# Counted V chunks of a mixture layer: all in rounded halves, twenty-two closing rows, first row reads one by one

## The chip, the cores and the metric

The program runs on one core of a Trainium2 chip. What is measured is the device time of one execution in microseconds (us); the time of a kernel is the median of several runs. The engines are TensorE (PE, with its weight loads as PEld), VectorE (DVE), ScalarE (ACT), GpSimd (POOL) and SyncE (SP, which here only issues transfers). The core has 16 DMA engines.

## The reference

One encoder layer on 256 tokens of width 2048 and one final norm. The change touches only the last sublayer and the end of the program: PEER, a mixture of 16,384 single-neuron experts. Eight product-key heads choose 16 experts each per token; an expert is a row u of one table and a row v of another:

```python
def block(args):
    xb, eb, gb = args
    u = u_tab[eb]
    act = jax.nn.gelu(jnp.einsum('td,tkd->tk', xb, u).astype(jnp.float32))
    return jnp.einsum('tk,tkd->td', (gb * act).astype(xb.dtype), v_tab[eb])
...
h = h + peer_ffn(rms_norm(h, ffn_norm_g), peer_w_q, peer_sub_keys, peer_u, peer_v)
...
return rms_norm(h, final_norm_g)
```

So a token's result is the sum over its 128 experts of gate x gelu(u . x) x v, added to h, and then normed.

## The kernel before

The retention and recurrent groups, the cross-attention and the routing fill the first half of the program. The expert layer is done in two ways at once. **Dense:** some experts are computed for all 256 tokens on TensorE, with gates that are zero where a token did not choose them: 40 rows of 128 experts fixed by number (U and V, in NCH = 5 chunks of 8 columns of 128 experts) and 32 columns of 128 that the kernel counts as the most chosen (the *counted* columns, NDY = 4 chunks, numbers 5 to 8; their rows are fetched from the tables by index, through `dyn`). **By row:** what is left of a token's choice, 38 rows for each of the two token halves (BASE = 38, tt = 0 and 1), is gathered by index: one transfer of 128 x 2048 f32 (1 MB) brings one row for each of 128 tokens. VectorE takes the dot products with u (`dot`, line 1508) and later accumulates coefficient x v into the output `hh` (`axpy`, line 1516). Choices that overflow the 38 are packed into two spill rows.

**The dense part** is one list of steps that `run` works through: U steps for all chunks, then V chunks in the order ORDER = (0, 1, 2, 3, 5, 6, 7, 8, 4). The last of them, chunk 4, is done by `v_final`. A V step normally works in rounded halves: ScalarE casts 1024 columns of the weight row to a reduced f32 form (`hi`, line 1422), VectorE forms the rest (`lo`, line 1442), and TensorE does three products, activations-hi x hi, activations-lo x hi and activations-hi x lo (`r_mms`, lines 1243, 1244 and 1246, for a counted chunk). The activations are split in the same way ahead of the chunk (`prep_steps`: `rounded` on ScalarE, line 1360, `left` on VectorE, line 1364, two of each per chunk). Chunks named in PLAIN skip all of that: `p_mms` (line 1252) multiplies the f32 activations with the f32 row as it came. There are four buffers `hi` and three `lo`. `given(n)` hands the activation buffer of a chunk that is through to the readers of counted rows (`rows_v`) or to the gathers (`ring`).

**The row work** runs beside the steps: after each step `wv.pump(rate)` adds a credit, and the generator `chosen` spends 2.2 of it per row. The rate is RP = 2.0 for a plain step and RR = 1.3 for a rounded step of a counted chunk. Of the 76 accumulations the last END, all of tt = 1, are set aside as *closing* rows: `ending` gives them out in `v_final`, whose loop of 12 tiles takes 18, between TensorE's products of chunk 4. The sums of TensorE's accumulators into `hh` are line 1694 (`added`, three quarters of the width) and line 1728 (the last quarter, once per token half, after TensorE's last product of that half); then the norm: squares on ScalarE (line 1670), a product with the gain on GpSimd (1719) and VectorE (1731), a reduction and a reciprocal root (1732, 217 to 224), a scaling (1740 on VectorE, 1736 on ScalarE) and the output's transfers.

**First reads.** While the last U columns of the early chunks run (line 164), VectorE finishes the choice of columns and rows (`compact`). When the second token half has been looked up, `first_reads` (line 1040) puts five transfers of 1 MB in a row on GpSimd's queue: the first normed rows `hn` into h[0], the first three counted U rows (two `row` tiles and h[1]), and the second normed rows into `held_in[8]`, which is `kept[3]`. Three gathers for the row work (`ahead`) were issued just before. The copies of one column ahead of each read (line 1044) tie the read to VectorE's order. After that come the products that pack the spill rows (`off`, line 1081; `spill`, line 1110, twice), and `rest()`, a branch on the chip for tokens that overflow further.

All engines work their instructions off in a fixed order, which the scheduler sets from the order in which the code was written and its own costs, except in stretches under `manual_schedule` (the steps, and the closing loop).

## Time and profile before

| | |
|---|---|
| median of 3 runs | 1923.39 us (1921.18 to 1926.32) |
| the profiled execution | 1924.19 us, span 1922.4 us, mean granted clock 0.990 |
| TensorE / VectorE / ScalarE / GpSimd busy | 97% / 80% / 45% / 29% of the span |
| first reads on GpSimd's queue | 1165.7 to 1179.5 us from the span's start |
| chunk 5 (plain), TensorE | 1665.4 to 1720.4 us |
| chunk 4 with the closing rows | from 1850.97 us |
| TensorE's last product ends | about 1912.8 us |

Times in the prediction's rows are microseconds from the span's start. A timeline row gives start, length, engine, line, instruction, output<-inputs, shape, count, and in brackets how long the engine had been idle before it and what released it. A row of a group gives busy us and mean ns of one, then the idle time before them. Line numbers are those of before unless "after" is said; from line 1040 on, after's numbers are two higher through most of the code (lines 1042 to 1110 differ by up to three).

### The profile page before, as it was taken

The page shows a single profiled execution, that of the slowest core. Times are in us where ns is not written, and L with a number is a line of the kernel's source. Part 1 is how long each engine was busy: PE and PEld are TensorE (multiplying, and loading weights), DVE is VectorE, ACT ScalarE, POOL GpSimd, SP SyncE. Part 2 cuts the span into 40 slices and gives each one's busy share as a digit, 9 for nine tenths or more (in the row PEclk, how much of TensorE's full clock was granted, in tenths as well). Part 3 has the DMA queues.
Part 4 walks back from the last instruction along what each step waited for, and adds up shares of the span by engine and source line. Part 5 has one row for each costly group of instructions (what it writes and reads, how often), then busy time and mean ns, then how long its engine had stood idle before and what let it go on. Part 6 is the DMA issues. An engine that isn't in the chain of part 4 may idle for free.

```text
span 1922.4 us, 28682 instructions
## 1 busy us (share of the span) xinstructions
PE 1871.8 (97%) x10698; PEld 1590.8 (83%) x10698; DVE 1529.1 (80%) x2336; ACT 871.9 (45%) x1340; POOL 550.7 (29%) x372
## 2 busy tenths in 40 slices
PE   9999999999999999999999998899999999899997
PEld 8888888888888988889999998888988787558863
DVE  6877979754556655799998887799999998689976
ACT  6567444544455555555347761333333433214411
POOL 0200010000000000000004641455553777388852
PEclk9999999999999999999999998999999999999999
DMA  8775665466665446855567999799898999899993
GB/s 286 287 214 170 214 212 168 155 184 192 194 180 165 149 154 187 294 166 175 200 220 175 189 245 314 269 372 387 305 408 319 353 393 412 327 367 398 420 411 134
DMA packets 202815, 498.03 MB, mean 259 GB/s; under 512 B 107040, under 2 KB 112800, under 8 KB 174624
## 3 DMA queue, kind: packets, MB, share of 16 engines
q1 hardware_dynamic: 163552, 261.57, 43.8%
q0 software_dynamic: 36384, 225.61, 29.8%
q10 hardware_dynamic: 2736, 8.99, 1.3%
q8 instruction: 84, 1.38, 0.3%
q14 instruction: 59, 0.48, 0.1%
HBM read 505.34 MB, written 21.04 MB: 274 GB/s over the span
## 4 chain that ended last, share of the span: by engine, by line
PE 68%; DMA 14%; DVE 9%; issue 5%; POOL 2%; ACT 1%; SPq 0%; POOLq 0%; DVEq 0%; ACTq 0%
PE wb L153 9%; PE xc L206 7%; PE xc L207 7%; PE xc L209 7%; PE wb L155 5%; PE U L164 5%; DMA gs<-in_Us_dram,idx 4%; PE acc L1252 3%; PE acc L1688 3%; PE G L1180 3%; DVE lo L144 3%; DMA kept<-in_V_dram 3%; DMA h<-in_Us_dram,dyn 2%; PE acc L1243 2%; PE acc L1244 2%
## 5 line engine op out<-in xcount | busy, mean ns | idle before, releaser
L144 DVE TENSOR_TENSOR lo<-raw,hi 128x1024 fp32r<-128x1024 f32 x364 | 443.8, 1221 | 213.1 <-PE xc L209 120.7
L143 ACT CAST hi<-raw 128x1024 fp32r<-128x1024 f32 x364 | 381.8, 1052 | 372.5 <-PE xc L207 170.9
L164 PE MATMUL U<-xn,hi 128*128 128x256 f32 x1280 | 176.4, 290 | 7.7 <-ACT hi L143 7.7
L164 PEld LDWEIGHTS U<-xn,hi 128*128 128x128 f32 x1280 | 164.4, 197 | 8.6 <-ACT hi L143 8.6
L804 POOL DMA_DIRECT2D hn<-h x2 | 1.1, 561 | 508.6 <-DVE h L802 508.6
L153 PE MATMUL U<-xn,hi 128*128 128x512 f32 x512 | 139.1, 404 | 0.2 <-DVE foldu L1285 0.2
L1422 ACT CAST hi<-kept 128x1024 fp32r<-128x1024 f32 x58 | 60.5, 1053 | 137.1 <-DMA at<-in_Vs_dram,idx 45.9
L153 PE MATMUL wb<-hT,hi 128*128 128x512 f32 x448 | 116.9, 396 | 0.5 <-ACT hi L143 0.5
L1167 POOL TENSOR_TENSOR kept<-kept 128x512 f32<-128x512 bf16 x64 | 73.9, 1155 | 108.4 <-DVE kept L1166 107.9
L153 PEld LDWEIGHTS U<-xn,hi 128*128 128x128 f32 x512 | 92.0, 190 | 15.7 <-DVE foldu L1285 0.5
L1508 DVE SCALAR_TENSOR_TENSOR junk<-gs,h 128x2048 bf16<-128x2048 f32 x43 | 98.2, 2283 | 6.4 <-DMA gs<-in_Us_dram,idx 6.2
L164 PE MATMUL U<-xn,lo 128*128 128x256 f32 x640 | 92.2, 287 | 4.9 <-DVE lo L144 4.7
L153 PEld LDWEIGHTS wb<-hT,hi 128*128 128x128 f32 x448 | 80.6, 189 | 14.7 <-ACT hi L143 0.7
L153 PE MATMUL wb<-xT,hi 128*128 128x512 f32 x352 | 89.2, 394 | 0.2 <-ACT hi L143 0.2
L164 PEld LDWEIGHTS U<-xn,lo 128*128 128x128 f32 x640 | 82.8, 193 | 7.7 <-DVE lo L144 7.3
L1439 DVE TENSOR_TENSOR lo<-uT,hi 128x512 fp32r<-128x512 f32 x128 | 81.9, 682 | 8.1 <-ACT hi L1420 7.2
L1501 POOL DMA_INDIRECT gs<-in_Us_dram,idx x51 | 60.0, 1177 | 79.1 <-DVE junk L1508 71.8
L1166 DVE TENSOR_TENSOR kept<-kept,kept 128x512 bf16<-128x512 bf16 x128 | 75.3, 636 | 7.5 <-PE cnt L1183 6.7
L1230 PE MATMUL acc<-hi,xe 128*128 128x512 f32 x192 | 77.7, 405 | 3.2 <-ACT hi L1422 3.1
L1516 DVE SCALAR_TENSOR_TENSOR hh<-gs,coef,hh 128x2048 f32<-128x2048 f32 x30 | 70.5, 2350 | 8.3 <-DMA gs<-in_Vs_dram,idx 8.1
L1442 DVE TENSOR_TENSOR lo<-kept,hi 128x1024 fp32r<-128x1024 f32 x58 | 69.6, 1221 | 9.3 <-ACT hi L1422 6.2
L1231 PE MATMUL acc<-hi,xe 128*128 128x512 f32 x192 | 77.0, 401 | 0.0
(532 smaller groups left out, 4603.9 us busy)
## 6 DMA issues: line engine op xcount, KB each, us to landing
raw<-in_U_dram SPq DMA_DIRECT2D x64, 512.0 KB, 3.7
raw<-in_w_qkv_dram SPq DMA_DIRECT2D x48, 512.0 KB, 4.2
raw<-in_w_xyg_dram SPq DMA_DIRECT2D x44, 512.0 KB, 4.5
raw<-in_V_dram SPq DMA_DIRECT2D x44, 512.0 KB, 11.9
raw<-in_w_xk_dram SPq DMA_DIRECT2D x32, 512.0 KB, 4.0
raw<-in_w_xv_dram SPq DMA_DIRECT2D x32, 512.0 KB, 4.2
raw<-in_w_out_dram SPq DMA_DIRECT2D x32, 512.0 KB, 4.1
raw<-in_w_xq_dram SPq DMA_DIRECT2D x32, 512.0 KB, 3.6
```

Of the source, the lines that this page charges most:

```text
L143: A.copy(hi, raw)
L144: V.tensor_tensor(lo, raw, hi.bitcast(F32), op=ALU.subtract)
L153: PE.matmul(pt, hi[:, ks], xt[:, kb, :], start=(kb == 0), stop=(kb == KB - 1))
L155: PE.matmul(pt[:, :T], lo[:, ks], xt[:, kb, :T], start=False, stop=False)
L164: PE.matmul(pt[:, :T], (lo if part == 2 else hi)[:, k * P:(k + 1) * P], x, start=(part == 0 and kb == 0), stop=(part == 2 and kb == KB - 1))
L206: PE.matmul(pt, xh, hi[:, w], start=(n == 0 and k == 0), stop=False)
L207: PE.matmul(pt, xl, hi[:, w], start=False, stop=False)
L209: PE.matmul(pt, xh, lo[:, w], start=False, stop=(n == 7 and k == 1))
L1230: PE.matmul(pt, ah[:, c, t_], hi[:, w], start=(first and c == 0), stop=False)
L1231: PE.matmul(pt, al[:, c, t_], hi[:, w], start=False, stop=False)
L1439: V.tensor_tensor(los[t][:, s], pts[t][n], his[t][:, s].bitcast(F32), op=ALU.subtract)
L1508: V.scalar_tensor_tensor(lefts[0] if lefts else junk, gat, 1.0, h[0] if rows is None else rows, op0=ALU.mult, op1=ALU.mult, accum_out=coef ...
```

## The change

Three edits. PLAIN loses chunk 5, so that all four counted V chunks go in rounded halves; by the same rule chunk 5's activation buffer is handed on at the end of the chunk before it. END goes from 18 to 22, so that four rows more are accumulated in `v_final`, behind its loop. `first_reads` keeps only the first normed rows; each of the first three counted U rows is read by `first_row` where the spill rows are packed, the first behind the copy of `off`, the others behind the copy of `ls` of each spill pass; and the read of the second normed rows is written behind `rest()`.

```diff
-PLAIN = (4, 5)
-END = 18
+PLAIN = (4,)
+END = 22
...
     def first_reads():
-        rows = [slot("qs", [P, D], f"row{n}") for n in range(2)] + [h[1]]
-        again = (h[0], held_in[NCH + NDY - 1])
-        for t in (h[0], *rows, again[1]):
-            V.tensor_copy(t[:, :1], key[1][:, :1])
+        V.tensor_copy(h[0][:, :1], key[1][:, :1])
         G.dma_start(h[0], hn[:P, :])
-        first_rows.extend(fetch(r, a["Us"], NS, dyn[:, n:n + 1]) for n, r in enumerate(rows))
-        G.dma_start(again[1], hn[P:2 * P, :])
+
+    def first_row(n, mark):
+        r = h[1] if n == 2 else slot("qs", [P, D], f"row{n}")
+        V.tensor_copy(r[:, :1], mark)
+        first_rows.append(fetch(r, a["Us"], NS, dyn[:, n:n + 1]))
...
         V.tensor_copy(off, pt[:, :TT])
+        first_row(0, off[:, :1])
         V.tensor_tensor(end, off, cnt_, op=ALU.add)
...
             V.tensor_copy(spl["t"][:, bs], ls[:, 2 * OVK:2 * OVK + 1])
+            first_row(1 + b, ls[:, :1])
             w1 = pgt.tile([P, 4], F32, tag="w1", name="w1")
...
     rest()
+    G.dma_start(held_in[NCH + NDY - 1], hn[P:2 * P, :])
     lefts.clear()
```

On GpSimd, at the first reads, before (`at` and `gs` are the three gathers ahead, `h` from `hn` the first normed rows, `row` and `h` from `Us` the counted rows, `kept_7761` from `hn` the second normed rows, `spti` the spill tokens):

```order
L1501 DMA at<-in_Us_dram,idx 128x2048
L1501 DMA gs<-in_Us_dram,idx 128x2048 x2
L1045 DMA h_4231<-hn 128x2048
L1501 DMA row_11545<-in_Us_dram,dyn 128x2048
L1501 DMA row_11546<-in_Us_dram,dyn 128x2048
L1501 DMA h_4232<-in_Us_dram,dyn 128x2048
L1047 DMA kept_7761<-hn 128x2048
L1501 DMA kept_7759<-hn,spti 128x2048
L1501 DMA at<-in_Us_dram,idx 128x2048
```

The same place on GpSimd after:

```order
L1800 DMA kept_7761<-hn 128x2048
L1503 DMA at<-in_Us_dram,idx 128x2048
L1503 DMA gs<-in_Us_dram,idx 128x2048 x2
L1042 DMA h_4231<-hn 128x2048
L1503 DMA row_11693<-in_Us_dram,dyn 128x2048
L1503 DMA row_11755<-in_Us_dram,dyn 128x2048
L1503 DMA kept_7759<-hn,spti 128x2048
L1503 DMA at<-in_Us_dram,idx 128x2048
L1503 DMA h_4232<-in_Us_dram,dyn 128x2048
L1503 DMA kept_7760<-hn,spti 128x2048
L1503 DMA gs<-in_Us_dram,idx 128x2048
L1631 TENSOR_LOAD many
```

The second normed rows, though written behind the branch (which begins with the load of `many`), now stand ahead of all the others, and the third counted row stands behind the first spill tokens and one more gather.

On VectorE, at the opening of chunk 5 after (`raw` and the first `kept_7762` are weights of chunk 3; `kept_7763`, `h_4232` and the later `kept_7762` are the first three counted rows; lines 1518 accumulate gathered rows):

```order
L1354 TENSOR_TENSOR kept_7761<-kept_7764,kept_7761 128x2048
L1444 TENSOR_TENSOR lo<-kept_7762,hi 128x1024
L1518 SCALAR_TENSOR_TENSOR hh_16905<-kept_7765,coef,hh_16905 128x2048
L1444 TENSOR_TENSOR lo<-kept_7762,hi 128x1024
L1444 TENSOR_TENSOR lo<-kept_7763,hi 128x1024 x2
L1518 SCALAR_TENSOR_TENSOR hh_16905<-gs,coef,hh_16905 128x2048
L1444 TENSOR_TENSOR lo<-h_4232,hi 128x1024
L1518 SCALAR_TENSOR_TENSOR hh_16905<-gs,coef,hh_16905 128x2048
L1444 TENSOR_TENSOR lo<-h_4232,hi 128x1024
L1444 TENSOR_TENSOR lo<-kept_7762,hi 128x1024
L1518 SCALAR_TENSOR_TENSOR hh_16905<-at,coef,hh_16905 128x2048
L1444 TENSOR_TENSOR lo<-kept_7762,hi 128x1024
```

Before, only accumulations stood behind the low halves of `kept_7762`, apart from two steps that round activations; now five low halves of counted rows stand ahead of the accumulation of `at`, and all others behind it.

On VectorE, at the end of the program, after (`hh_16905` is the first token half and `hh_16906` the second; `acc` with its number is a TensorE accumulator):

```order
L1518 SCALAR_TENSOR_TENSOR hh_16906<-h_4231,coef,hh_16906 128x2048
L1730 TENSOR_TENSOR hh_16905<-hh_16905,acc_16515 128x512
L1733 TENSOR_TENSOR fin<-hh_16905,fg 128x512
L1518 SCALAR_TENSOR_TENSOR hh_16906<-gs,coef,hh_16906 128x2048
L1518 SCALAR_TENSOR_TENSOR hh_16906<-kept_7759,coef,hh_16906 128x2048
L1518 SCALAR_TENSOR_TENSOR hh_16906<-kept_7760,coef,hh_16906 128x2048
L1518 SCALAR_TENSOR_TENSOR hh_16906<-kept_7765,coef,hh_16906 128x2048
L1696 TENSOR_TENSOR hh_16905<-hh_16905,acc_16513 128x512
L1696 TENSOR_TENSOR hh_16906<-hh_16906,acc_16514 128x512
L1730 TENSOR_TENSOR hh_16906<-hh_16906,acc_16516 128x512
```

Before, all eighteen accumulations and the two sums of line 1694 stood ahead of line 1728; now the first token half's last sum (line 1730) and its product with the gain stand ahead of the last four accumulations, and the sums of line 1696 behind these.

## The prediction

> **What bounds the kernel now.** I read the page's busy shares and the chain that ended last, then the windows by stage, then TensorE's timeline where the change touches it, and for each of its waits the engine that released it. From the page's first part and the end of the chain:
>
> ```profile
> PE 1871.8 (97%) x10698; PEld 1590.8 (83%) x10698; DVE 1529.1 (80%) x2336; ACT 871.9 (45%) x1340; POOL 550.7 (29%) x372
> ```
> ```profile
> 1665.45 54.93 PE acc L1252 x128
> ...
> 1905.05 6.87 PE acc L1688 x16
> ```
>
> TensorE works for 97% of the span; 1922.4 - 1871.8 = 50.6 us are left. So a part of the change counts if it takes products off TensorE, takes away one of its few waits, or lengthens what follows its last product. The first counted V chunk (chunk 5), in plain f32 products, is one unbroken link of 54.93 us. Three windows (busy us and instructions of PE, PEld, DVE, ACT, POOL; granted clock, DMA share, GB/s):
>
> ```profile
> 1180.00:1200.00 20.00, 15.54 (x95) 15.06 (x96) 8.72 (x35) 3.42 (x4) 0.07 (x1) 0.68 1.00 401
> ```
> ```profile
> 1665.00:1720.00 55.00, 55.00 (x131) 24.53 (x130) 36.73 (x19) 3.24 (x4) 43.66 (x25) 1.00 0.96 373
> 1720.00:1850.00 130.00, 130.00 (x574) 107.45 (x573) 123.79 (x85) 53.00 (x53) 109.75 (x54) 1.00 0.98 400
> ```
>
> From 1180 to 1200, during the first reads, the DMA engines are full and TensorE works 15.54 of 20 us at a mean clock of 0.68. The second row is chunk 5: VectorE is idle for 55.00 - 36.73 = 18.3 us of it. The third is chunks 6 to 8, in rounded halves already: TensorE never stops, but VectorE has only 130.00 - 123.79 = 6.2 us to spare in three chunks, and the DMA engines are at 0.98. Chunk 5 is to become like these.
>
> **First reads.** TensorE's timeline, and one row of ScalarE's:
>
> ```profile
> 1179.82 3.78 PE L164 MATMUL U<-xn,hi 128*128 128x256 f32 x16 [2.76 <-ACT hi L143]
> 1187.35 3.79 PE L164 MATMUL U<-xn,hi 128*128 128x256 f32 x16 [3.75 <-ACT hi L143]
> ...
> 1192.87 2.08 PE L164 MATMUL U<-xn,hi 128*128 128x256 f32 x16
> ...
> 1198.55 0.37 PE L1110 MATMUL spill<-ov,own 128*128 128x18 f32 x2 [0.72 <-DVE own L1096]
> ...
> 1204.75 0.37 PE L1110 MATMUL spill<-ov,own 128*128 128x18 f32 x2 [3.18 <-DVE w L1121]
> ...
> 1206.50 3.47 PE L164 MATMUL U<-xn,hi 128*128 128x256 f32 x16
> ...
> 1225.80 3.71 PE L1411 MATMUL uT<-ident,row 128*128 128x128 f32 x32 [0.47 <-ACT kept L1218]
> ```
> ```profile
> 1201.71 1.04 ACT L143 CAST hi<-raw 128x1024 fp32r<-128x1024 f32 x1 [5.61 <-DMA raw<-in_U_dram]
> ```
>
> Two long waits come before 1187.35, three shorter ones after it, and sixteen products take 3.5 to 3.8 us after a wait instead of 2.08. The 3.18 us put down to VectorE is a transfer's: the cast that VectorE's rounding follows waited 5.61 us for a U block. GpSimd's queue and the landings at that time:
>
> ```profile
> 1165.71 1.04 POOL L1501 DMA_INDIRECT at<-in_Us_dram,idx  x1 [22.87 <-DVE ov L1078]
> ...
> 1174.97 0.58 POOL L1045 DMA_DIRECT2D h<-hn  x1 [5.13 <-DVE sel L949]
> ...
> 1179.49 0.58 POOL L1047 DMA_DIRECT2D kept<-hn  x1
> ```
> ```profile
> q0 software_dynamic: 393, 2.88, 69.0%
> ...
> h<-hn POOLq DMA_DIRECT2D x1, 1024.0 KB, 11.0
> kept<-hn POOLq DMA_DIRECT2D x1, 1024.0 KB, 19.6
> ```
>
> Eight transfers of 1 MB are issued from 1165.71 to 1179.49; from 1175 to 1185 their queue takes 69% of the engines' time. h<-hn, fourth of them, lands 11.0 us after its issue, at 1186; kept<-hn, the last, at 1199. The change leaves the first four together, so both waits up to 1187.35 stay. The three rows come later, one at a time, and the second normed rows go ahead of all eight: between 1187 and 1199 the U blocks meet at most one of the four. What can go is 0.72 + 3.18 + (3.47 - 2.08) + 0.47 = 5.8 us. The spill products keep a chain of small VectorE steps between them, and three of the new column copies stand in it, so I take 4.5 off; ends 0 and 5.8. The rows are first used at 1225.80, over 20 us after the last spill product, and landed in 11 to 20 us: I cost their delay at nothing, and at a few us if the third is issued behind two gathers.
>
> **Chunk 5 in rounded halves.** In chunk 6 the same four products recur at every step:
>
> ```profile
> 1722.06 1.07 PE L1246 MATMUL acc<-lo,xe 128*128 128x512 f32 x4
> ...
> 1724.78 1.07 PE L1246 MATMUL acc<-lo,xe 128*128 128x512 f32 x4
> ```
> ```profile
> L1442 DVE TENSOR_TENSOR lo<-kept,hi 128x1024 fp32r<-128x1024 f32 x38 | 45.5, 1222 | 3.1 <-PE acc L1246 3.1
> L1516 DVE SCALAR_TENSOR_TENSOR hh<-gs,coef,hh 128x2048 f32<-128x2048 f32 x18 | 42.3, 2349 | 6.5 <-DMA gs<-in_Vs_dram,idx 6.3
> ```
>
> A step takes 2.72 us, a chunk 16 x 2.72 = 43.5, so TensorE saves 54.93 - 43.5 = 11.4 us. ScalarE's casts fit beside (53.00 of 130 us). VectorE gets 16 low halves and two roundings, 18 x 1.22 = 22.0 us. A plain step gave the row work a credit of 2.0, a rounded one gives 1.3, and an accumulation costs 2.2: 16 x 2.0 / 2.2 = 14.5 accumulations become 9.5, 5.1 x 2.35 = 12.0 us fewer. VectorE then has 36.73 + 22.0 - 12.0 = 46.7 us of work in a stage of 43.5, and waits for rows on top. The opening of chunk 5 on three engines (VectorE, GpSimd, TensorE):
>
> ```profile
> 1676.97 2.35 DVE L1516 SCALAR_TENSOR_TENSOR hh<-at,coef,hh 128x2048 f32<-128x2048 f32 x1 [9.05 <-DMA at<-in_Vs_dram,idx]
> ```
> ```profile
> 1663.54 2.86 POOL L1318 DMA_INDIRECT kept<-in_Vs_dram,dyn  x1 [12.03 <-DVE lo L1442]
> ...
> 1670.38 0.99 POOL L1501 DMA_INDIRECT kept<-in_Vs_dram,idx  x1 [0.30 <-issue]
> ```
> ```profile
> 1659.93 1.83 PE L1233 MATMUL acc<-lo,xe 128*128 128x512 f32 x4 [2.02 <-DVE lo L1442]
> ```
>
> GpSimd is held for 12.03 us by a buffer, and VectorE then waits 9.05 us for the row issued behind it. In plain products nobody felt it; now low halves that TensorE needs stand behind that accumulation. With w for VectorE's waits for rows, and two low halves (5.4 us) made ahead, TensorE is late by 46.7 + w - 5.4 - 43.5 = w - 2.2. If rows land when they do now, the 10.0 us of added work fill part of the 18.3 idle: w = 8.3, late by 6.1. Following the order row by row, the row at 1676.97 costs only 1.4: 1676.97 + 2.35 + 1.22 = 1680.5 for a half wanted at 1665.45 + 5 x 2.72 = 1679.1, plus an added rounding of 1.2 where TensorE already waited 2.02 at 1659.93: 2.6. Between 2.6 and 6.1 I take 4 (ends 0, and w = 18.3, late by 16): 11.4 - 4 = 7.4 off.
>
> **The closing rows.** VectorE's end, ScalarE's and GpSimd's first closing steps, and the DMA engines then:
>
> ```profile
> 1897.36 2.35 DVE L1516 SCALAR_TENSOR_TENSOR hh<-h,coef,hh 128x2048 f32<-128x2048 f32 x1
> 1899.63 1.28 DVE L1694 TENSOR_TENSOR hh<-hh,acc 128x512 f32<-128x512 f32 x2
> 1905.08 0.69 DVE L1728 TENSOR_TENSOR hh<-hh,acc 128x512 f32<-128x512 f32 x1 [4.17 <-PE acc L1727]
> 1905.81 0.69 DVE L1731 TENSOR_TENSOR fin<-hh,fg 128x512 f32<-128x512 f32 x1
> ...
> 1908.22 1.28 DVE L1740 TENSOR_SCALAR hh<-hh,rf 128x512 f32<-128x512 f32 x3
> 1912.81 0.69 DVE L1728 TENSOR_TENSOR hh<-hh,acc 128x512 f32<-128x512 f32 x1 [3.31 <-PE acc L1727]
> ```
> ```profile
> 1900.44 0.61 ACT L1670 ACTIVATE fin<-hh 128x512 f32<-128x512 f32 x1
> ```
> ```profile
> 1880.00:1890.00 10.00, 10.00 (x25) 4.50 (x24) 9.00 (x6) 0.72 (x2) 7.20 (x4) 1.00 0.52 205
> ```
>
> Eighteen accumulations now end at 1899.63, and VectorE idles 4.17 us for TensorE's last sum of the first token half. The order shows that sum and its scaling (lines 1730 and 1733 after) ahead of the last four accumulations. In this clock: VectorE still waits to 1905.08, is through both at 1906.5, the four rows take 4 x 2.35 = 9.4 to 1915.9, two sums 1.28 to 1917.2; there the second half's last sum starts, 4.4 us later than at 1912.81. All second-half squares now come behind the last row: five at 0.61 us and a little between them hold ScalarE to 1919.3, where the last square could start at 1917.9: 1.4 more; and the first half's three scalings (1.28) now stand before the second half's last step. So 4.4 + 1.4 + 1.3 = 7.1 later. The rows themselves are there (four more MB fit behind 1885, where the engines fall to 0.52). Ends: 4.4, and 10 if VectorE reaches the closing rows 2.9 us late.
>
> **Sum.** -4.5 - 7.4 + 7.1 = -4.8 against the profiled execution's 1924.19 (its span 1922.4, and 1.8 around it): 1919.4. That execution lies 0.8 above the median 1923.39, so 1918.6 beside the median.
>
> **The rivals.**
> Forecast: as worked out, 1915 to 1922.
> A, the waits go in full: 5.8 off at the reads, chunk 5 late by only 1.2, the tail only 4.4: -5.8 - 10.2 + 4.4 = -11.6, so 1911.8. For it: low halves of chunk 5 have a row in hand earlier, since its act buffer is released a chunk sooner. Against: the 12.03 us hold.
> B, GpSimd paces chunk 5. One row of GpSimd while VectorE works without pause:
>
> ```profile
> 1751.55 3.10 POOL L1318 DMA_INDIRECT kept<-in_Vs_dram,dyn  x1 [0.30 <-DVE lo L1442]
> ```
>
> An issue is 0.99 us at 1670.38 with VectorE idle, and 3.10 here. In chunks 6 to 8, 54 issues take 109.75 + 54 x 0.30 = 126 of 130 us, 2.33 each. Chunk 5 needs 8 + 9.5 of them, 40.8 us, behind the hold of 12.03: 52.8, a gain of 2.1 instead of 7.4: 1923.9. For it: the row work of these chunks keeps GpSimd full; against: TensorE never waited there. The Trainium skill, page "SBUF — State Buffer", section "Who interferes with whom", has a rule that speaks against the change here: a VectorE instruction with two SBUF inputs and a GpSimd instruction that reads SBUF lock each other out for a whole instruction. The 3.10 beside the 0.99 agrees with it, and by it the eighteen added two-input instructions would lead to B.
> C, slower: VectorE becomes the bound from chunk 5 to the end. It decides where its waits for rows pass 2.2 us, and is worse than before where they pass 13.6. With all 18.3 kept, chunk 5 is late by 16.1 - 11.4 = 4.7 net, VectorE comes late to the closing rows (10), the reads give 4.5: +10.2, so 1933.6. For it: 6.2 us to spare in 130. Against: waits shrink when the engine comes later.
> D, the reads give nothing: the branch is no barrier for the second normed rows (the order has them first on GpSimd), and the rows still meet U blocks. -7.4 + 7.1: 1923.1.
>
> **How the numbers follow.** Forecast 0.42, A 0.22, B 0.13, C 0.11, D 0.12. A measurement of this kernel tells about 0.3%, 5.8 us, from no change: faster is below 1917.6, slower above 1929.2. The forecast's own range straddles 1917.6, with 0.4 of it below. Faster: 0.22 + 0.17 + 0.01 of the others = 0.40; slower: C and a little of B, 0.13; same 0.47. For 8 in 10 the range goes from 1910, under A, to 1928, leaving out C and the edges.
>
> **What would show it.** After: an unbroken chunk 5 of about 47 to 48 us with TensorE waits for low halves in its first half; no TensorE wait over 1 us between 1190 and 1210, both earlier ones still there; VectorE's line 1730 before four accumulations, and the last line 224 about 7 us further behind TensorE's last product. Chunk 5 near 44 is A; near 53 with GpSimd never idle is B; VectorE without pause and TensorE waiting in chunks 6 to 8 is C. It is wrong altogether if the time moves in a stage not named here.

## The result, and the profile after

The changed kernel takes 1932.56 us (median of 20 runs, 1925.30 to 1940.01). The kernel before, run on the same chip, takes 1921.19 (20 runs, 1917.12 to 1926.32). The ratio is 1.006, with a 95% interval of 1.005 to 1.0069: slower by 11.4 us (9.6 to 13.3). That lies above the predicted range and on the other side of no change. The profiled execution of the changed kernel took 1933.48 us, with a span of 1931.1.

The stages of the two profiled executions, in us, each from one start in TensorE's or VectorE's timeline to the next:

| stage | before | after | difference | predicted |
|---|---|---|---|---|
| start to the product for `off` (line 1081) | 1191.6 | 1187.0 | -4.6 | 0 |
| to the first transposes `uT` (first reads) | 34.2 | 28.7 | -5.5 | -4.5 |
| to the first V product | 243.7 | 250.5 | +6.8 | 0 |
| V chunks up to chunk 5 | 195.8 | 197.7 | +1.9 | 0 |
| chunks 5 to 8 | 185.5 | 181.4 | -4.1 | -7.4 |
| chunk 4, to TensorE's last product | 62.0 | 62.0 | 0 | 0 |
| from there to the last line 224 | 3.1 | 16.8 | +13.7 | +7.1 |
| the output | 6.6 | 7.1 | +0.5 | 0 |

The differences add up to the spans' 8.7. Executions of the kernel before differ among themselves by up to 17 us (1913.43 to 1930.62 in the batches below), and single profiles show part of that in stages that no edit touches: 3.7 of the first row's 4.6 lie ahead of the first reads. So a stage difference of a few us in one pair of profiles proves nothing alone; what is read off below was seen again in other kernels with the same part. From the page's first part after:

```profile
PE 1860.9 (96%) x10762; PEld 1602.0 (83%) x10762; DVE 1551.4 (80%) x2353; ACT 890.5 (46%) x1358; POOL 541.9 (28%) x372
```

TensorE works 10.9 us less than before (1871.8), nearly the 11.4 that were worked out, and yet the span is longer: TensorE's idle time grew from 50.6 to 70.2 us. Three windows after, in the columns of the prediction's windows, show where:

```profile
1660.00:1720.00 60.00, 55.53 (x227) 44.28 (x227) 49.81 (x33) 21.20 (x21) 45.81 (x24) 0.94 0.89 353
1720.00:1850.00 130.00, 130.00 (x566) 105.81 (x565) 120.67 (x83) 50.14 (x50) 101.25 (x51) 1.00 0.92 361
...
1915.00:1935.00 20.00, 0.00 (x0) 0.00 (x0) 9.54 (x25) 5.42 (x16) 5.38 (x4) 0.53 0.29 106
```

Chunk 5 has gaps now (55.53 of 60). The chunks behind it have none, but their DMA engines moved 361 GB/s where they moved 400. And after 1915 TensorE is through, while VectorE, ScalarE and GpSimd still have 9.54, 5.42 and 5.38 us of work. TensorE's waits at the opening of chunk 5, after:

```profile
1657.43 2.07 PE L1235 MATMUL acc<-lo,xe 128*128 128x512 f32 x4 [3.02 <-DVE lo L1444]
1679.80 1.20 PE L1248 MATMUL acc<-lo,xe 128*128 128x512 f32 x4 [0.33 <-DVE lo L1444]
1686.03 1.20 PE L1248 MATMUL acc<-lo,xe 128*128 128x512 f32 x4 [0.50 <-DVE lo L1444]
1690.69 1.20 PE L1248 MATMUL acc<-lo,xe 128*128 128x512 f32 x4 [1.64 <-DVE lo L1444]
1706.59 1.22 PE L1248 MATMUL acc<-lo,xe 128*128 128x512 f32 x4 [1.99 <-DVE lo L1444]
```

Inside chunk 5 it waits 0.33 + 0.50 + 1.64 + 1.99 = 4.5 us for low halves. VectorE's end, after:

```profile
1883.91 2.35 DVE L1518 SCALAR_TENSOR_TENSOR hh<-h,coef,hh 128x2048 f32<-128x2048 f32 x1 [1.43 <-DMA h<-in_Vs_dram,idx]
1887.72 2.35 DVE L1518 SCALAR_TENSOR_TENSOR hh<-gs,coef,hh 128x2048 f32<-128x2048 f32 x1 [1.45 <-DMA gs<-in_Vs_dram,idx]
...
1903.26 0.68 DVE L1730 TENSOR_TENSOR hh<-hh,acc 128x512 f32<-128x512 f32 x1
1903.97 1.05 DVE L1733 TENSOR_TENSOR fin<-hh,fg 128x512 f32<-128x512 f32 x1
1904.95 3.35 DVE L1518 SCALAR_TENSOR_TENSOR hh<-gs,coef,hh 128x2048 f32<-128x2048 f32 x1
1908.33 7.13 DVE L1518 SCALAR_TENSOR_TENSOR hh<-kept,coef,hh 128x2048 f32<-128x2048 f32 x3
...
1916.57 0.68 DVE L1730 TENSOR_TENSOR hh<-hh,acc 128x512 f32<-128x512 f32 x1
...
1919.35 1.18 DVE L222 TENSOR_TENSOR rq_s<-rq_s,rq_m 128x1 f32<-128x1 f32 x1
...
1920.75 1.00 DVE L224 TENSOR_TENSOR rf<-rf,rq_s 128x1 f32<-128x1 f32 x1
```

The order is the predicted one: line 1730, line 1733, four accumulations, the second half's last sum. But line 1730 at 1903.26 no longer waits for TensorE (4.17 us before): VectorE arrives last. It comes from closing rows that are 3.8 us apart, each with 1.4 us of waiting for its transfer. The last two gathers that GpSimd issued before, and then, after, the first closing gather, the eighteenth and the last two:

```profile
1879.92 0.99 POOL L1501 DMA_INDIRECT kept<-in_Vs_dram,idx  x1 [2.46 <-DVE hh L1516]
1883.38 0.99 POOL L1501 DMA_INDIRECT h<-in_Vs_dram,idx  x1 [2.47 <-DVE hh L1516]
```
```profile
1834.13 0.98 POOL L1503 DMA_INDIRECT gs<-in_Vs_dram,idx  x1 [9.28 <-issue]
...
1886.54 0.99 POOL L1503 DMA_INDIRECT h<-in_Vs_dram,idx  x1 [2.80 <-DVE hh L1518]
...
1897.22 2.21 POOL L1503 DMA_INDIRECT kept<-in_Vs_dram,idx  x1 [0.30 <-issue]
1899.74 2.08 POOL L1503 DMA_INDIRECT kept<-in_Vs_dram,idx  x1 [0.30 <-PE acc L1729]
```

Chunk 4 starts at 1850.81 before and at 1845.27 after, so the last row is asked for 32.6 us into chunk 4 before and 54.5 us into it after. TensorE came 5.5 us earlier to chunk 4, and the last row was asked for 16 us later: 3.2 us by the eighteenth closing row, the last one before (1886.54 against 1883.38), and 13.2 by the four rows more. In the meantime the DMA engines, at 0.52 from 1880 to 1890 before, have no room left after:

```profile
1880.00:1890.00 10.00, 10.00 (x25) 4.47 (x24) 6.99 (x4) 0.00 (x0) 1.98 (x2) 1.00 1.01 404
```

Where the rows were displaced is shown by the accumulations alone (VectorE's busy us and their number, in windows of the row accumulation's line), before and then after:

```profile
1660.00:1720.00 60.00, 37.36 (x16) 0.97 0.88 342
...
1885.00:1915.00 30.00, 13.34 (x6) 1.00 0.16 61
```
```profile
1660.00:1720.00 60.00, 25.71 (x11) 0.94 0.89 353
...
1885.00:1915.00 30.00, 25.32 (x11) 0.96 0.38 141
```

Five accumulations fewer beside chunk 5, five more at the very end; in between the counts agree within one. The 54.93 us of plain products had been the cover under which VectorE, GpSimd and the DMA engines got ahead with rows.

### The profile page after: what moved, and what is told of

It is laid out like the page before. It is cut to its first block, busy times and chain, and to the rows that moved or that the text cites. A ratio compares the mean times of both kernels' runs of the same rounds, so it can differ in the third digit from the quotient of the medians.

```text
span 1931.1 us, 28864 instructions
## 1 busy us (share of the span) xinstructions
PE 1860.9 (96%) x10762; PEld 1602.0 (83%) x10762; DVE 1551.4 (80%) x2353; ACT 890.5 (46%) x1358; POOL 541.9 (28%) x372
## 4 chain that ended last, share of the span: by engine, by line
PE 65%; DMA 15%; DVE 11%; issue 7%; POOL 2%; ACT 1%; SPq 0%; POOLq 0%; DVEq 0%; ACTq 0%
PE wb L153 10%; PE xc L206 7%; PE xc L207 7%; PE xc L209 7%; PE wb L155 5%; PE U L164 4%; DMA kept<-in_Vs_dram,idx 4%; PE G L1182 3%; PE U L153 3%; DVE lo L144 2%; DMA kept<-in_V_dram 2%; DMA gs<-in_Us_dram,idx 2%; PE acc L1245 2%; PE acc L1246 2%; PE acc L1248 2%
## 5 line engine op out<-in xcount | busy, mean ns | idle before, releaser
L1424 ACT CAST hi<-kept 128x1024 fp32r<-128x1024 f32 x70 | 73.2, 1053 | 118.4 <-PE acc L1246 59.1
L1245 PE MATMUL acc<-hi,xe 128*128 128x512 f32 x256 | 100.6, 393 | 0.0
L1246 PE MATMUL acc<-hi,xe 128*128 128x512 f32 x256 | 100.6, 393 | 0.0
L1444 DVE TENSOR_TENSOR lo<-kept,hi 128x1024 fp32r<-128x1024 f32 x70 | 83.7, 1217 | 5.4 <-ACT hi L1424 4.9
L1518 DVE SCALAR_TENSOR_TENSOR hh<-kept,coef,hh 128x2048 f32<-128x2048 f32 x31 | 72.8, 2348 | 16.7 <-DMA kept<-in_Vs_dram,idx 16.5
```

The source lines that it names most:

```text
L1245: PE.matmul(pt, ah[:, c, t_], hi[:, w], start=False, stop=False)
L1246: PE.matmul(pt, al[:, c, t_], hi[:, w], start=False, stop=False)
L1444: V.tensor_tensor(los[t], part_of(t), his[t].bitcast(F32), op=ALU.subtract)
```

## The experiments

The first theory after this result, **rows**: the gathered rows, not TensorE, set the end, and the shorter chunk 5 takes away their time. Its rivals: VectorE's added low halves do it; the closing count does it; the rounded form itself costs time. Differences in us below are the recorded ratio less one, times 1921; that ratio is not exactly the quotient of the two medians.

**One part of the change at a time.** Rounding alone, on the kernel before:

```diff
-PLAIN = (4, 5)
+PLAIN = (4,)
```

> The kernel before with chunk 5 in rounded halves alone; 18 closing rows, old first reads. Theory ROWS (the row transfers and accumulations are the bound behind chunk 3, and TensorE's time saved in chunk 5 comes back at the end, since about four rows that no longer fit beside chunk 5 are left over for the end): TensorE reaches chunk 4 some 4 us earlier, the end comes 8 to 12 us further behind that point; +3 to +8 us in all. Theory FOUR (the rounding pays by itself, and only the four closing rows behind TensorE's last sum cost): -4 to -8 us.

Measured 1936.41 us, ratio 1.008 (1.0063 to 1.0097), 15 us slower, about twice the most that theory ROWS had allowed. Chunks 5 to 8 take 180.6 us in its profile, 4.9 less than before; the end from TensorE's last product to the last line 224 takes 17.0 instead of 3.1. It has 18 closing rows, so the long end is not due to their count: rows of the sweep that were not done now stand behind the last low half.

The closing rows alone, on the kernel before:

```diff
-END = 18
+END = 22
```

> The kernel before with 22 closing rows alone. Theory ROWS: the number of rows that are behind when chunk 4 begins is what counts, and with plain chunk 5 the rows set aside are simply fetched later through the same full DMA engines: -1 to +4 us. Theory FOUR: four rows of 2.35 us behind the last sum and the squares behind them: +5 to +9 us.

Measured 1924.68, ratio 1.0017 (1.0004 to 1.003), 3.3 us slower, with an end of 5.3 us, 2.2 longer. In the order that the scheduler gives this kernel only one accumulation stands behind line 1728 of the first half, so it does not test the four that stand there in the changed kernel.

The reads alone, from the changed kernel:

```diff
-PLAIN = (4,)
-END = 22
+PLAIN = (4, 5)
+END = 18
```

> The changed kernel's first reads alone, chunk 5 plain and 18 closing rows. Theory ROWS: TensorE is 5 to 7 us earlier at the first counted column, loses 4 to 6 us there waiting for the later rows, and the rest is swallowed where the DMA engines are full from 1500 on: -2 to +1 us. The prediction's own step: -4.5 us.

Measured 1918.57, ratio 0.9991 (0.9979 to 1.0004): -1.7 us, not told from no change.

The changed kernel with 18 closing rows:

```diff
-END = 22
+END = 18
```

> The changed kernel with 18 closing rows instead of 22. Theory ROWS: the four rows are left over from the sweep instead and drained ahead of the closing ones, so the end is about as late: +6 to +12 us against the kernel before, 0 to 4 below the changed kernel. Theory FOUR: the 7.1 us of the tail are gone and the kernel is 4 to 8 us faster than before.

Measured 1932.29, ratio 1.0047 (1.0032 to 1.0063), 9 us above before. Its end takes 17.8 us. With chunk 5 rounded, 18 or 22 closing rows make no large difference. This kernel and the reads alone differ in chunk 5's form only: 0.9991 against 1.0047 is 10.8 us, a second measurement of what the rounding costs by itself.

Half of chunk 5, on the kernel before: columns 4 to 7 rounded, 0 to 3 plain.

```diff
-                    yield Step("R", None if half else column(c),
-                               lambda row, c=c, half=half: p_mms(acts[i], row, c, half), RP, half, plain=True)
+                    if c < 4:
+                        yield Step("R", None if half else column(c),
+                                   lambda row, c=c, half=half: p_mms(acts[i], row, c, half), RP, half, plain=True)
+                    else:
+                        yield Step("R", None if half else column(c),
+                                   lambda hi, lo, c=c, half=half: r_mms(*ahs[i], hi, lo, c, half), RR, half)
...
+        if i in PLAIN and i >= NCH:
+            def begin_half():
...
+                rounded(1)
+            return reads, {1 + gap: [(begin_half, None)], 1 + 2 * gap: [(None, lambda: left(1))]}
```

> The kernel before with only columns 4 to 7 of chunk 5 in rounded halves (8 low halves and one rounding on VectorE, 11 us; TensorE saves 5.7 us). Theory VECTOR: VectorE's idle time in the plain chunk (18 us) takes most of it, but the rows that no longer fit come back at the end: 0 to +6 us against the kernel before. Theory TRANSFERS: rows are asked for at nearly the old rate, -3 to +2 us.

Measured 1926.77, ratio 1.0016 (1.0 to 1.0032), 3 us slower. This one point between brings no gain either. Chunks 5 to 8 take 188.7 us there, more than before, with TensorE busy for only 17.06 of the 20 us from 1830 to 1850, at a clock of 0.83; so it does not show what half the saving would be worth without that.

**What holds the end.** Chunk 5's 16 low halves on VectorE are left out; TensorE multiplies the high half in their place (`thin` marks the steps of chunk 5), so that the product's small part is missing there:

```diff
...
+            elif steps[t].thin:
+                los[t] = his[t]
```

> The changed kernel without the sixteen low halves that VectorE makes for chunk 5 (18 us of VectorE's work; TensorE still does its twelve products a step, with the high half in the low half's place, so the computation loses the low part of chunk 5's rows). Theory VECTOR (from chunk 5 on VectorE's added work is the bound): chunk 5 to chunk 4 takes 175 us instead of 181, the tail is 8 or more shorter, and the kernel is 12 to 16 us faster than the changed one. Theory TRANSFERS (the row transfers behind chunk 3 are the bound, however busy VectorE is): TensorE is earlier by 6, the tail longer by as much, 0 to 4 us faster than the changed kernel.

Measured 1929.43, ratio 1.0047 (1.0025 to 1.0068): still 9 us above before. VectorE in chunk 5, in this kernel:

```profile
1672.41 2.35 DVE L1520 SCALAR_TENSOR_TENSOR hh<-at,coef,hh 128x2048 f32<-128x2048 f32 x1 [8.98 <-DMA at<-in_Vs_dram,idx]
1677.39 2.35 DVE L1520 SCALAR_TENSOR_TENSOR hh<-kept,coef,hh 128x2048 f32<-128x2048 f32 x1 [2.62 <-DMA kept<-in_Vs_dram,idx]
...
1687.77 2.35 DVE L1520 SCALAR_TENSOR_TENSOR hh<-gs,coef,hh 128x2048 f32<-128x2048 f32 x1 [3.19 <-DMA gs<-in_Vs_dram,idx]
...
1698.70 2.35 DVE L1520 SCALAR_TENSOR_TENSOR hh<-kept,coef,hh 128x2048 f32<-128x2048 f32 x1 [2.64 <-DMA kept<-in_Vs_dram,idx]
```

With 16 x 1.22 = 19.5 us less to do, VectorE simply waits for rows. Chunks 5 to 8 take 175.7 us, so the product saving was sized rightly (185.5 - 11.4 = 174.1), and TensorE reaches chunk 4 at 1836.5, where the changed kernel reached it at 1845.3; but the end grows from 16.8 to 20.5 us. Of the 5.7 us that TensorE gains in these chunks the end takes back about 3.8: the rows set it, and the low halves of chunk 5 do not. The time, about 2.5 us below the changed kernel with intervals that overlap, is in the range of theory TRANSFERS and far from that of VECTOR.

Four of the 22 closing rows are not fetched (their accumulations use an old tile, so those four rows are missing from the output):

```diff
-                held.append(fetch(free[m % len(free)], a["Vs"], NS, idx[tt][:, k:k + 1]))
+                if 6 <= m < 10:
+                    held.append(held[m - len(free)])
+                else:
+                    held.append(fetch(free[m % len(free)], a["Vs"], NS, idx[tt][:, k:k + 1]))
```

> The changed kernel, in which the closing rows 6 to 9 are not read: the accumulations are all there and take the row that lies in their buffer, so four wrong rows are added and 4 MB less are moved. Theory VECTOR: 0 to 3 us faster than the changed kernel. Theory TRANSFERS: the waits of 1.4 us ahead of each closing row are gone sooner, 8 to 12 us faster.

Measured 1926.12, ratio 1.0024 (1.0006 to 1.0042): about 7 us below the changed kernel, with the same work for VectorE: under the 8 to 12 of theory TRANSFERS, but well over the 0 to 3 of VECTOR.

The last four closing rows are fetched but not added:

```diff
-                axpy(tt, k, held[m - deep])
+                if m - deep < len(closing) - 4:
+                    axpy(tt, k, held[m - deep])
```

> The changed kernel without the accumulation of the last four closing rows, which are still read. Both theories: 9 to 11 us faster than the changed kernel, since these four stand behind the last sum; under 5 us would mean that the end hangs on the transfers of those rows.

Measured 1926.59, ratio 1.0035 (1.0021 to 1.005): about 5 us below. Their four accumulations are 9.4 us of VectorE, and only half of that comes off, where 9 to 11 were expected. The intervals of these two trials overlap; together they suggest that fetching a row costs here at least about what adding it costs.

The buffer that held GpSimd for 9.28 us at 1834.13 is the one that the sweep used last (accumulated from 1830.71); `ring` gave it out first. Here it comes last:

```diff
-        ring[:] = loose[TT:] + [b for b in ring if any(b is t for t in kept)]
+        ring[:] = [b for b in ring if any(b is t for t in kept)] + loose[TT:]
```

> The changed kernel with one line more: the gather buffer that the sweep used last comes last and not first in the ring of the closing rows, so that GpSimd doesn't stand 9.3 us in front of the first closing gather. Theory TRANSFERS: nearly all of these 9 us go from the end, 6 to 9 us faster than the changed kernel, -1 to +6 against the kernel before. Theory VECTOR: VectorE has the same work, 0 to 3 us faster than the changed kernel.

Measured 1928.64, ratio 1.0038 (1.002 to 1.0056): about 4 us below the changed kernel, with intervals that just overlap, and between what the two theories expected. GpSimd and the end of VectorE in this kernel:

```profile
1835.53 1.73 POOL L1503 DMA_INDIRECT gs<-in_Vs_dram,idx  x1 [1.67 <-DVE hh L1518]
```
```profile
1899.78 0.69 DVE L1730 TENSOR_TENSOR hh<-hh,acc 128x512 f32<-128x512 f32 x1 [0.63 <-PE acc L1729]
...
1901.11 9.51 DVE L1518 SCALAR_TENSOR_TENSOR hh<-kept,coef,hh 128x2048 f32<-128x2048 f32 x4
```

The hold shrinks to 1.67 us, VectorE waits for TensorE again at line 1730, and the end takes 11.7 us. That is the situation the prediction described. From 1830 to 1840 this kernel moves 405 GB/s; the changed kernel moved 193.

Two variants of it. Two rows per tile in the first ten tiles of the closing loop:

```diff
-                for _ in range(1 + t % 2):
+                for _ in range(2 if t < 10 else 1):
```

> As g1_ring, and the closing loop gives out all twenty-two rows (two per tile for ten tiles), so that fewer stand behind the first half's last sum. If the four rows behind that sum cost what the prediction said: 3 to 6 us faster than g1_ring. If the end hangs on when the last row lands: within 2 us of it.

Measured 1926.58, ratio 1.0023 (1.0006 to 1.004). And counted rows asked for two steps later:

```diff
-            while cool and cool[0][0] + 2 <= clock[0]:
+            while cool and cool[0][0] + 4 <= clock[0]:
```

> As g1_ring, and a counted row's buffer is handed to its next read four steps after its last use instead of two, so that GpSimd's reads of counted V rows stand later in its queue and hold up fewer gathers. Theory TRANSFERS: the 11.6 us hold ahead of chunk 5 gets shorter, 2 to 6 us faster than g1_ring, or slower where a counted row then comes late for TensorE. Theory VECTOR: within 2 us of g1_ring.

Measured 1928.09, ratio 1.0033 (1.0014 to 1.0052). Neither is told from the kernel with the new buffer order; an end of 12.6 us stays in both. In the second, GpSimd's hold ahead of chunk 5 is 11.35 us, against 11.04 without this edit: it was not shortened, and that trial says little.

**Does the rounded form itself cost time?** Twelve of the 58 rows of the sweep (the accumulations that are not closing rows) are left out, neither fetched nor added, and missing from the output, in the kernel before and in the one with rounding alone (what the second text calls column chunk 4's pair is chunk 5):

```diff
+        moves = moves[:30] + moves[42:]
```

> The kernel before with 12 of its 58 sweep rows left out (neither read nor accumulated, so that these rows are missing from the output): the row transfers should then not be what ends last. Both theories: TensorE's stages as before (chunk 5 about 195 us long by the mark from the first V product, the tail from TensorE's last product to the last L224 about 3 us), total 1910 to 1924 us, since TensorE with its waits set the end of the kernel before already. If it comes far below 1905, rows held TensorE too in the kernel before.

> The kernel before with column chunk 4's pair rounded in halves as in e1_plain, and the same 12 sweep rows left out as in h1. Theory ROWS (rounding loses in the changed kernel only because the row transfers then end last): with 12 rows fewer the saved TensorE time shows, the tail from TensorE's last product to the last L224 stays under 6 us, and the time is 6 to 11 us below that of h1. Theory ROUNDING (the rounded form itself costs time, on VectorE or by its readiness): the time is that of h1 or above it, by up to 15 us as e1_plain was above the kernel before.

Unrounded: 1927.79, ratio 1.0032 (1.0018 to 1.0046). Rounded: 1916.86, ratio 0.9979 (0.9967 to 0.9991), 10.9 us below it. The end of VectorE in the rounded one:

```profile
1891.30 0.69 DVE L1695 TENSOR_TENSOR hh<-hh,acc 128x512 f32<-128x512 f32 x1
...
1907.61 0.69 DVE L1729 TENSOR_TENSOR hh<-hh,acc 128x512 f32<-128x512 f32 x1 [2.96 <-PE acc L1728]
```

VectorE is early again and waits 2.96 us for TensorE; the end takes 3.07 us, where it was 16.96 with the same rounding and all rows. Twelve rows fewer move the rounded kernel from 1.008 to 0.9979, about 19 us, and bring the unrounded one nothing. So the rounding loses because rows end last. A row that is left out takes its gather, its transfer and its accumulation with it, so that these two kernels do not say which of the three is slowest; the one with four rows not fetched speaks for the first two. The pair's own difference is not the worth of the rounding, though: the unrounded one missed its expectation, being slower than before with less work. Its TensorE stood here:

```profile
1743.23 1.20 PE L1246 MATMUL acc<-lo,xe 128*128 128x512 f32 x4 [3.50 <-DVE lo L1442]
```

for a low half behind an accumulation that had waited 4.84 us for `at`, and the clock was 0.83 in the ten us around it; why `at` came later there than before was not followed up. Against the kernel before, the rounding with twelve rows fewer is worth 4 us, not 7.4 and not 11.4: chunks 5 to 8 take 182.0 us in it.

**Where the reads' 5.5 us went.** After, the transposes start at 1215.69 instead of 1225.80, and then a wait stands in them that before does not have. TensorE, and the instructions of the branch (line 1632; length min/median/max in ns, first and last start), after:

```profile
1182.76 3.79 PE L164 MATMUL U<-xn,hi 128*128 128x256 f32 x16 [3.70 <-ACT hi L143]
...
1215.69 3.27 PE L1413 MATMUL uT<-ident,row 128*128 128x128 f32 x28 [0.47 <-ACT kept L1220]
1224.07 1.12 PE L1413 MATMUL uT<-ident,row 128*128 128x128 f32 x4 [5.10 <-DVE lo L1441]
```
```profile
L1632 POOLq EVENT_SEMAPHORE  x4: 17/42/43, 1218.7 to 1222.7; - x4
...
L1632 DVEq COMPARE_BRANCH  x1: 72/72/72, 1217.7 to 1217.7; - x1
...
L1632 DVEq EVENT_SEMAPHORE  x1: 21/21/21, 1223.2 to 1223.2; - x1
```

VectorE enters the branch at 1217.7, skips its body, and is let out at 1223.2, after GpSimd has passed its last semaphore there at 1222.7. GpSimd's last gather ahead of the branch was issued at 1208.88 and landed 13.6 us later, at 1222.5. The same holds in two other kernels: before, the last one was issued at 1214.90 and landed 8.6 us later, at 1223.5, and the last semaphore is at 1223.7; with the reads alone, 1210.18 + 13.2 = 1223.4, and 1223.6. In the kernel with the early third row (below), whose trace has no landing, the DMA engines fall silent between 1220.1 and 1220.6, and the last semaphore is at 1220.4. So it is inferred that the branch waits for GpSimd's transfers. Its end hardly moved (the chain that ended last has it at 1224.6 before and 1223.5 after), and what TensorE won ahead of it was lost at it. The third counted row, read before the second pass and not behind two gathers, on the reads alone:

```diff
-            first_row(1 + b, ls[:, :1])
+            if not b:
+                first_row(1, ls[:, :1])
+                first_row(2, ls[:, :1])
```

> As e3_reads, with the third counted row read behind the first spill pass like the second. If the 5.1 us wait at the first counted columns is that row's: the wait goes and the kernel is 1 to 4 us faster than e3_reads, -7 to -3 against the kernel before. If the relief is swallowed later in any case: within 1 us of e3_reads.

Measured 1917.30, ratio 0.9978 (0.9964 to 0.9992), 4.2 us below the kernel before; the wait is 2.64 us, half of what it was and not gone. The reads alone without the branch (work for tokens that overflow further is left out):

```diff
-    rest()
+    rest
```

> e3_reads (only the first reads of the changed kernel) without the branch for tokens that overflow further (the call of rest() is left out, so the work for such tokens is missing). Theory BRANCH (the reads do free 5.5 us, and TensorE then meets the branch, which GpSimd leaves only when its transfers have landed, at about 1223 us, and which holds VectorE until then): the wait of 5.28 us in the transposes of the counted rows goes or falls under 1.5 us, and the time is 3 to 7 us below that of e3_reads, that is 1912 to 1916. Rival TRANSFERS (the third counted row and the gathers themselves are late; the branch only shows it): the wait stays at 3 us or more behind another releaser, and the time is that of e3_reads, 1917 to 1921.

Measured 1915.40, ratio 0.9974 (0.9961 to 0.9987), 5.0 us below before. In TensorE's timeline the 32 transposes are one piece, without the wait:

```profile
1216.11 3.71 PE L1413 MATMUL uT<-ident,row 128*128 128x128 f32 x32 [0.47 <-ACT kept L1220]
```

The same edit on the kernel before:

> The kernel before without the same branch (the work for tokens that overflow further is left out), its first reads as they were. Theory BRANCH: in the kernel before, TensorE reaches the transposes at 1225.80, when the branch is through anyway, so that leaving it out gives little: 0 to 2 us, 1919 to 1922. If it gives 4 us or more, the branch costs time of its own and i1 must be read against this run, not against the kernel before.

Measured 1919.19, ratio 1.0003 (0.9987 to 1.0019): nothing. So the branch costs only where TensorE comes early to it, and it took about 3 us of what the reads freed (1.7 gained with it, 5.0 without; these intervals overlap a little, but the wait is there in the one profile and gone in the other).

Last, the early third row together with the new buffer order:

> g4_rows_early (unrounded chunk 5, 18 closing rows, the third counted row read early) with the gather buffers of the closing rows in the order of g1_ring. In the kernel before GpSimd does not stand at that place for long (4.40 us at 1846.67, against 9.28 in the changed kernel), and its tail is TensorE's 3.06: no change against g4, 1915 to 1919. If rows hold the end there too, 2 to 4 us less.

Measured 1918.20, ratio 0.9993 (0.998 to 1.0007). The buffer order adds nothing where chunk 5 is plain. The two kernels differ by 2.9 us, with intervals that overlap; the early third row is the best whole kernel measured, by less than the 0.3% that the prediction set as its bound.

## Why the prediction was wrong, step by step

**Products of chunk 5, -11.4: right.** TensorE's busy time fell by 10.9, and without the low halves chunks 5 to 8 came to within 1.6 us of the full saving.

**Chunk 5 late by 4: mis-sized.** The formula held and its input did not: late by w - 2.2, with w VectorE's waits for rows. VectorE's accumulations in chunk 5, after:

```profile
1676.26 2.35 DVE L1518 SCALAR_TENSOR_TENSOR hh<-at,coef,hh 128x2048 f32<-128x2048 f32 x1 [5.28 <-DMA at<-in_Vs_dram,idx]
...
1682.49 2.35 DVE L1518 SCALAR_TENSOR_TENSOR hh<-kept,coef,hh 128x2048 f32<-128x2048 f32 x1 [1.61 <-DMA kept<-in_Vs_dram,idx]
...
1687.14 2.35 DVE L1518 SCALAR_TENSOR_TENSOR hh<-gs,coef,hh 128x2048 f32<-128x2048 f32 x1 [1.17 <-DMA gs<-in_Vs_dram,idx]
...
1692.02 2.35 DVE L1518 SCALAR_TENSOR_TENSOR hh<-gs,coef,hh 128x2048 f32<-128x2048 f32 x1 [0.26 <-DMA gs<-in_Vs_dram,idx]
...
1703.05 2.35 DVE L1518 SCALAR_TENSOR_TENSOR hh<-kept,coef,hh 128x2048 f32<-128x2048 f32 x1 [1.87 <-DMA kept<-in_Vs_dram,idx]
```

It waits 5.28 + 1.61 + 1.17 + 0.26 + 1.87 = 10.2 us, which gives 8.0; TensorE was 181.4 - 174.1 = 7.3 late (4.5 of it the waits shown above), and the two other kernels with all counted chunks rounded and no buffer edit gave 6.0 and 6.5. I had followed the one long wait at 1676.97 and let the others vanish in the added work. They did not: rows came later as VectorE came later. On GpSimd's queue a counted row stands now between almost every two gathered rows; that a faster TensorE asks for counted rows sooner is the likely reason.

**The closing rows, +7.1: the step that failed.** "The rows themselves are there (four more MB fit behind 1885, where the engines fall to 0.52)". The number of displaced rows was right: the credits take 5.1 accumulations from chunk 5, and five are missing there. What failed is that their fetching was put at nothing. I read the DMA engines' room off the end of the kernel before, as if the rows that now stand there would not fill it: from 1880 to 1890 the engines are at 1.01, not at 0.52, the closing rows come 3.8 us apart, and a hold of 9.28 us at 1834.13 lets the engines fall to 193 GB/s just ahead of them. The last four rows did not keep VectorE waiting; the eighteen ahead of them did. Of the 6.6 us between 13.7 and 7.1, 3.7 are line 1730, which comes 58.0 us into chunk 4 instead of the 54.3 assumed (VectorE arrives behind its rows, not behind TensorE). Another 1.2 lie between the two lines 1730, 13.3 us apart instead of the 12.1 worked out, since the four accumulations and line 1733 take longer than alone (10.5 against 9.4, 1.05 against 0.69). The rest, 1.7, is about what lines 222 and 224 take more, 1.18 and 1.00 us where they had 0.16. With the buffer order mended, the first of these is gone and the end is 11.7, against 3.1 + 7.1 = 10.2. Measured alone, the rounding costs 15.4 us where the two terms on chunk 5 had it gain 7.4.

**The reads, -4.5: right where it was looked for, lost at the next place.** Both early waits stayed and the later ones went (-5.5), but measured alone the reads gain 1.7 us, not told from nothing. The cost of delayed counted rows at nothing was not the error; I had not asked what TensorE would run into 5.5 us sooner. It was the branch.

**The rivals.** The mechanism nearest to the result is C, and its time, 1933.6, is nearly that measured, which is luck: it has chunk 5 at +4.7 and the reads at -4.5, and neither came so. Its condition, waits of more than 2.2 us, was met, and VectorE came late to the closing rows (3.7, against 2.9 in its bound). But VectorE's load in chunk 5 was not the bound, as the kernel without the low halves shows; and chunk 5 did not lose more than it saved (7.3 of 11.4): most of the loss lies at the end. In the chunks behind, after, VectorE never waits for a row from 1708 to 1834 and pauses there for 1.17 us at most; GpSimd issues one row after another from 1708.84 to 1824.85, never more than 0.54 us apart; the DMA engines are at 0.79 from 1720 to 1750 and full only later. So the transfers do not set the pace of the accumulations there; VectorE does, or GpSimd with it, and no run separates the two. TensorE waits for neither.

B fell as the pace of chunk 5: GpSimd stands for 4.60 us at 1706.81. The kernel without low halves passed the chunk at nearly full speed, but it says little against B, since its issues were shorter too (27 in 37.26 us from 1660 to 1720, against 24 in 45.81 after). The lock that the Trainium skill states (page "SBUF — State Buffer", section "Who interferes with whom") agrees with the trace at the very end, where an accumulation beside GpSimd's products of line 1721 took 3.35 us and not 2.35, and with how long an issue takes beside VectorE (last section).

The three edits measured singly add up to +15.4 + 3.3 - 1.7 = 17.0 and gave 11.4 together, so part of the cost is shared; how it is shared stays open. Open too is the stage ahead of chunk 5, which the prediction had at 0: the ten profiles with chunk 5 rounded in full take 194.2 to 197.7 us from the first V product to chunk 5, the seven with it plain and all rows 188.4 to 195.8, five of them under 191. So the rounding may cost some us there as well, which the table hides because the one profile of before is the slowest of the seven in this stage; no run tests it.

## What to carry to other kernels

A long stretch of plain products can be the cover for a second stream of work that has no slack of its own; before shortening it, count what that stream does under it (here 14 rows) and ask where those units will go. When an engine is freed early, look for the next place at which all engines meet, such as a branch on the chip, and for what ends it. An idle resource at the end of the profile before is not room for the change if the change moves work to just that place.

## What the runs showed of the chip that was not expected

A branch whose body is skipped held VectorE for 5.5 us (1217.7 to 1223.2): GpSimd leaves it only behind semaphores that it passed at 1218.7 to 1222.7, the last of them 0.2 us behind the landing of its youngest gather.

One buffer that is given out too early stops all gathers behind it: GpSimd stood 9.28 us before the gather at 1834.13, and the DMA engines fell to 193 GB/s from 1830 to 1840.

Products behind a wait can be slow, and the length of the wait alone does not say how slow. After, four products behind a wait of 3.02 us took 2.07 us, with a granted clock of 0.66 from 1655 to 1665; behind waits of 0.33 to 1.99 us they took 1.20 to 1.22. But sixteen products behind 3.19 us at 1176.89 took 2.18, with a clock of 1.00 from 1171 to 1181, where sixteen behind 3.70 us at 1182.76 took 3.79, with 0.66 from 1180 to 1190.

Very small VectorE steps are stretched beside GpSimd: lines 222 and 224, each 0.16 us before, took 1.18 and 1.00 us while GpSimd ran the four products of line 1721, 5.38 us from 1916.35.

A gather that GpSimd begins to issue while a VectorE instruction runs is held until that instruction ends. After:

```profile
1647.39 1.22 DVE L1444 TENSOR_TENSOR lo<-raw,hi 128x1024 fp32r<-128x1024 f32 x1
1647.75 1.73 POOL L1503 DMA_INDIRECT gs<-in_Vs_dram,idx  x1 [7.13 <-DVE hh L1518]
...
1882.75 0.99 POOL L1503 DMA_INDIRECT kept<-in_Vs_dram,idx  x1 [2.81 <-DVE hh L1518]
```

The first issue ends 0.87 us behind VectorE's instruction; the second begins while VectorE is idle. Of the 105 issues between 1600 and 1905 us, 27 began under no VectorE instruction and took 0.98 to 1.01 us each; 71 of the 78 others ended 0.84 to 0.89 us behind the end of one, most often after about 1.96 or 3.1 us. The seven left took 0.98 to 1.01 us: five began within 0.03 us of VectorE's instruction, and two stood beside line 1696, which reads one of its two inputs from a TensorE accumulator. VectorE's own instructions beside the issues kept their 1.22 and 2.35 us.
